# Attention probabilities of a hybrid encoder: one slot per head pair, turned as rounded words, values in one run

## The chip, the cores and the metric

The kernel runs on one core of a Trainium2 chip. The metric is the device time of one launch in microseconds (us); lower is better. TensorE (in profiles PE, its weight loads PEld) does the matmuls, VectorE is DVE, ScalarE is ACT, GpSimd is POOL, and SyncE (SP) issues the transfers. A float32 tile can also be declared as "rounded" words (F32R in the code, fp32r in a profile): the same four bytes, which TensorE takes in a cheaper kind of matmul. A plain float32 matmul of the program stands in the trace as two instructions, a rounded one and a transposition as one.

## The reference

One layer of an encoder is applied to two requests, 256 and 1024 rows of 2048 features. The input projection feeds three groups: a state-space scan (ssd), windowed attention, and attention to a memory of 256 rows per request. Their results are projected back and added to the input. The change touches the two attentions:

```python
# window attention: 8 heads of 64, 2 key-value heads, |t-s| <= 128, ALiBi, a sink logit per head
logits = where(valid, s - slopes * dist, -inf)
m = maximum(max(logits, axis=-1), sk)
pr = exp(logits - m)
probs = pr / (sum(pr, axis=-1) + exp(sk - m))
o = einsum('bngrqk,bnkgd->bnqgrd', probs, vw)
...
# memory attention: 4 heads of 128, 256 memory rows
pm = softmax(sm, axis=-1)
o_mem = einsum('bhtm,bmhd->bthd', pm, mv) * silu(z_mem)
```

## The kernel before

**Main work.** The projections are split-precision matmuls: each weight tile is split into a rounded part `wh` (ACT, L206) and the rest `wl` (DVE, L207), the inputs `xH` and `xL` likewise, and three rounded matmuls (L258 to L260, L293 to L295, L1268 to L1270) are summed into the PSUM tiles `acc`. Weights come by transfers into `wraw` tiles. Rows are worked in ten tiles of 128 (tiles 0 to 7 one request, 8 and 9 the other) in two groups of five.

**Work beside it.** Everything else is written as generators, put into two lanes (`queue`, L138). After each block step of a projection `pump` (L158) takes steps from the lanes, at rates by the name of the projection (RATES, L32). The attention tiles, key preparation and memory attention are in lane 0, the ssd work in lane 1. So the attention's matmuls come in short runs between the projection's matmuls, on the same TensorE queue, in about the order in which they are written; the weight splits have a higher priority. Three PSUM buffers (tag "mix", L74) serve all of the work beside the projections.

**Window attention, `attn(t)` (L620).** A tile of 128 query rows sees `na` blocks of 128 keys: two for tiles 0, 7, 8 and 9, three for the other six. For each of four head numbers `rr`, one head for each of two key-value heads `kv`:

- `scores(rr)` (L663): POOL copies the two sink logits into a column of the tile `lg` (L665). Two rounded matmuls per kv give the scores in PSUM (`psc`, L671 and L672), DVE adds the distances and takes the extreme value into `lg` (L673), ACT makes the exponentials with their sum (L677), DVE scales by half the reciprocal (L681).
- `turn_(rr)` (L685): for each kv, `na` transpositions of `lg` on TensorE, as plain float32 words against `ident`, into a PSUM tile `ppt` (L693); then ACT copies that to `pT` (L694), before the next kv's transpositions are written.
- `values(half)` (L698): for two `rr` together, plain float32 matmuls of `v_all` (64 columns, so the two kv fill the two halves of the PSUM partitions) with `pT`, 256 columns each (L703), then one DVE multiplication by the gate `z` (L706).

The order of steps is: scores 0, 1, turn 0, scores 2, turn 1, scores 3, values 0, turn 2, turn 3, values 1, with yields between. `lg` has two buffers that rotate, so scores 2 must wait until turn 0 has read its buffer; `pT` has one buffer for two `rr`.

**Memory attention, `mem_attn(t)` (L734),** is built alike with two head pairs `hp`: exponentials and scaling in `mpr` (L781, L786; the buffers of `lg`), four transpositions per `hp` (L794, plain words, PSUM tile `pmt`), an ACT copy to `mpT` (L798; the buffer of `pT`), and values for each `hp` (L809, 128 columns into all 128 partitions).

**Neighbours that the prediction uses.** The queries are turned as rounded words against `identr` (L653, PSUM tile `pq`, four to a run). The ssd work has plain matmuls of 128 columns into 64 partitions, the two halves of the partitions in turn, 32 instructions to a run (L970, PSUM tile `py`), and plain transpositions in fours (L1038, `pr`). `rsqrt` (L122) puts two small instructions on POOL. A table of row factors `rbc` for group 1 (L1463) also lives in a buffer of `lg`; it is last read at 603.7 us, ahead of the first transposition of `lg` at 637.5 us.

Of the kernel before, what the change touches and what calls it, by code (L numbers as in the profile page):

```python
# [10 lines left out]
F32 = mybir.dt.float32  # L11
F32R = mybir.dt.float32r
# [3 lines left out]
AF = mybir.ActivationFunctionType  # L16
ALU = mybir.AluOpType
AX = mybir.AxisListType

P = 128  # L20
# [24 lines left out]
def hymba_encoder_kernel(  # L45
# [37 lines left out]
    def psum(name):  # L83
        return mix.tile([P, 512], F32, tag="mix", name=name)
# [41 lines left out]
    def hv(ap, n=8):  # L126
        return ap.rearrange("p (h d) -> p h d", h=n)
# [48 lines left out]
    rbc = {}  # L176
# [440 lines left out]
        yield  # L617


    def attn(t):  # L620
        lo, hi = (0, NS) if t < NS else (NS, NT)
        k0, k1 = max(lo, t - 1), min(hi, t + 2)
        na = k1 - k0
        nk = na * P
        d0 = (k0 - (t - 1)) * P
        s0 = k0 if t < 4 else k0 - 3
        grp, ti = divmod(t, 5)
        tc_ = slice(ti * P, (ti + 1) * P)
        q = taken("attn", t)
        yield  # L630
        sq = w2("sq")
        A.activation(sq, q, AF.Square)
        ss = sm.tile([P, 8], F32, tag="s8", name="qss", bufs=4)
        V.reduce_sum(out=ss, in_=hv(sq), axis=AX.X)
        r = sm.tile([P, 8], F32, tag="s8", name="qr", bufs=4)
        rsqrt(r, ss, 1.0 / 64, 8)
        G.tensor_tensor(out=r, in0=r, in1=steep, op=ALU.mult)
        for _ in range(3):
            yield
        q3 = hv(q)  # L640
        V.tensor_mul(q3, q3, hb(r, 8, 64))
        yield
        qT = []
        for b in range(2):
            qh = mp.tile([P, 4, 2, 64], F32R, tag="wa", name="qh", bufs=WA)
            qb = q3[:, 4 * b:4 * b + 4, :]
            A.activation(qh[:, :, 0, :], qb, AF.Copy)
            V.tensor_sub(qh[:, :, 1, :], qb, qh[:, :, 0, :].bitcast(F32))
            yield
            ps = psum("pq")  # L650
            qf = qh.rearrange("p a b d -> p (a b d)")
            for a in range(4):
                T.transpose(ps[:, a * P:(a + 1) * P].bitcast(F32R), qf[:, a * P:(a + 1) * P], identr)  # L653
            o = mp.tile([P, 512], F32R, tag="qT", name="qT", bufs=2)
            A.activation(o, ps, AF.Copy)
            qT.append(o)
        z = w2("za")
        S.dma_start(hv(z, 4), zT_d[0][grp][:, :, tc_])
        yield
        ns8 = nsink.rearrange("p (v r) -> p r v", v=2)  # L660
        state_ = {}

        def scores(rr):  # L663
            lg = mp.tile([P, 2, 385], F32, tag="lg", name="lg", bufs=2)
            G.tensor_copy(lg[:, :, nk:nk + 1], ns8[:, rr, :].unsqueeze(2))  # L665
            nm = sm.tile([P, 2], F32, tag="m2", name="nm", bufs=10)
            for kv in range(2):
                h = 4 * kv + rr
                ps = psum("psc")
                st = qT[kv][:, rr * P:(rr + 1) * P]  # L670
                T.matmul(ps[:, :nk], st, kT[:, kv, s0 * P:s0 * P + nk], start=True, stop=False)  # L671
                T.matmul(ps[:, :nk], st, kL[:, kv, s0 * P:s0 * P + nk], start=False, stop=True)  # L672
                V.tensor_tensor_reduce(out=lg[:, kv, :nk], in0=pdist[:, d0:d0 + nk], in1=ps[:, :nk], scale=2.0 ** -(h + 1),  # L673
                                       scalar=nsink[:, h:h + 1], op0=ALU.add, op1=ALU.min, accum_out=nm[:, kv:kv + 1])
            den = sm.tile([P, 2], F32, tag="m2", name="den", bufs=10)
            for kv in range(2):
                A.activation(lg[:, kv, :nk + 1], lg[:, kv, :nk + 1], AF.Exp, scale=-1.0, bias=nm[:, kv:kv + 1],  # L677
                             accum_out=den[:, kv:kv + 1])
            V.reciprocal(out=den, in_=den)
            for kv in range(2):  # L680
                V.tensor_scalar(out=lg[:, kv, :nk], in0=lg[:, kv, :nk], scalar1=den[:, kv:kv + 1], scalar2=0.5,  # L681
                                op0=ALU.mult, op1=ALU.mult)
            state_[rr] = lg

        def turn_(rr):  # L685
            lg = state_.pop(rr)
            if rr % 2 == 0:
                state_["pT"] = mp.tile([P, 2, 2, 384], F32, tag="pT", name="pT", bufs=1)
            pT = state_["pT"]
            for kv in range(2):  # L690
                pt = psum("ppt")
                for a in range(na):
                    T.transpose(pt[:, a * P:(a + 1) * P], lg[:, kv, a * P:(a + 1) * P], ident)  # L693
                A.activation(pT[:, kv, rr % 2, :nk], pt[:, :nk], AF.Copy)  # L694

        oT = w2("oT")

        def values(half):  # L698
            pT = state_.pop("pT")
            po = psum("po")  # L700
            for a in range(na):
                for kv in range(2):
                    T.matmul(hv(po[kv * 64:kv * 64 + 64, :2 * P], 2), v_all[:, s0 + a, kv * 64:kv * 64 + 64],  # L703
                             pT[:, kv, :, a * P:(a + 1) * P], start=(a == 0), stop=(a == na - 1))
            c = slice(half * 2 * P, (half + 1) * 2 * P)
            V.tensor_mul(oT[:, c], po[:, :2 * P], z[:, c])  # L706

        scores(0)
        yield
        scores(1)  # L710
        yield
        yield
        turn_(0)
        yield
        scores(2)
        yield
        turn_(1)
        yield
        scores(3)
        yield  # L720
        values(0)
        yield
        turn_(2)
        yield
        turn_(3)
        yield
        fetch_next()
        yield
        values(1)
        yield  # L730
        S.dma_start(oT_d[0][grp][:, :, tc_], hv(oT, 4))


    def mem_attn(t):  # L734
# [31 lines left out]
        def scores(hp):  # L766
            ps = psum("pms")
            for j in range(2):
                h = 2 * hp + j
                c = slice(h * P, (h + 1) * P)  # L770
                o = ps[:, j * 256:(j + 1) * 256]
                T.matmul(o, qh[:, c], mkH[:, h, :], start=True, stop=False)
                T.matmul(o, qh[:, c], mkL[:, h, :], start=False, stop=False)
                T.matmul(o, ql[:, c], mkH[:, h, :], start=False, stop=True)
            m = sm.tile([P, 2], F32, tag="m2", name="mm", bufs=10)
            V.reduce_max(out=m, in_=hv(ps, 2), axis=AX.X)
            V.scalar_tensor_tensor(out=m, in0=m, scalar=-1.0, in1=r[:, 2 * hp:2 * hp + 2], op0=ALU.mult, op1=ALU.mult)
            pr = mp.tile([P, 512], F32, tag="lg", name="mpr", bufs=2)
            den = sm.tile([P, 2], F32, tag="m2", name="mden", bufs=10)
            for j in range(2):  # L780
                A.activation(pr[:, j * 256:(j + 1) * 256], ps[:, j * 256:(j + 1) * 256], AF.Exp,  # L781
                             scale=r[:, 2 * hp + j:2 * hp + j + 1], bias=m[:, j:j + 1], accum_out=den[:, j:j + 1])
            V.reciprocal(out=den, in_=den)
            for j in range(2):
                c = slice(j * 256, (j + 1) * 256)
                V.tensor_scalar(out=pr[:, c], in0=pr[:, c], scalar1=den[:, j:j + 1], scalar2=0.5,  # L786
                                op0=ALU.mult, op1=ALU.mult)
            st_[hp] = pr

        def turn_(hp):  # L790
            pr = st_[hp]
            pt = psum("pmt")
            for a in range(4):
                T.transpose(pt[:, a * P:(a + 1) * P], pr[:, a * P:(a + 1) * P], ident)  # L794
            if hp == 0:
                st_["pT"] = mp.tile([P, 2, 768], F32, tag="pT", name="mpT", bufs=1)
            pT = st_["pT"][:, hp, :512]
            A.activation(pT, pt, AF.Copy)  # L798
            st_[hp] = pT

# [658 lines left out]
    def x_rows(grp):  # L1459

        yield
        yield
        rbc[grp] = fin.tile([P, 640], F32, tag="rbc", name="rbc") if grp == 0 else \  # L1463
            mp.tile([P, 640], F32, tag="lg", name="rbc", bufs=2)
        for o, n in ((0, 4), (4, 1)):
            ps = psum("prx")
            for i in range(n):
                t = 5 * grp + o + i
                T.matmul(ps[:, i * P:(i + 1) * P], rx[:, t:t + 1].broadcast_to([P, P]), ident, start=True, stop=True)
            V.tensor_copy(rbc[grp][:, o * P:(o + n) * P], ps[:, :n * P])  # L1470
        yield
# [289 lines left out]
```

## Time and profile before

| | us |
|---|---|
| median of 3 runs | 1787.72 (1787.32 to 1790.27) |
| profiled execution, first to last instruction | 1784.2 |
| TensorE busy in it | 1774.6 |
| VectorE busy | 1245.8 |
| ScalarE busy | 921.5 |
| GpSimd busy | 547.3 |
| window attention's transpositions | 637.5 to 1303.8 |
| memory attention's transpositions | 828.6 to 1466.8 |

The profile describes one execution, whose own time isn't recorded beyond its span. In a timeline row the columns are: start in us from the span's start, duration in us, engine, line of the kernel, operation, the tile written and the tiles read, partitions and elements, and the count of merged instructions. Matmul durations overlap: the next one starts before the last one ends. In a row by groups, "busy, mean ns of one" stands behind the first bar, and behind the second the idle time of the engine just before these instructions with what ended it.

### The profile page before, as it was taken

What the parts mean: (1) busy time and instruction counts of PE and PEld (TensorE: products, weight loads), DVE (VectorE), ACT (ScalarE), POOL (GpSimd) and SP (SyncE); (2) the same over time, 40 slices, a digit from 0 to 9 for tenths busy, and PEclk for the clock granted to TensorE, in tenths of its full rate; (3) what the DMA queues carried; (4) which work ended last, traced back from release to release, by engine and by line L of the source; (5) the groups of instructions that cost most, each with busy time, mean ns of one, the idle gap of its engine ahead of it and who ended that gap; (6) DMA issues with size and microseconds to landing.
All of it is one profiled execution on the core that took longest, in us unless ns stands there. A gap on an engine that the chain in (4) does not pass through costs nothing.

```text
span 1784.2 us, 31407 instructions
## 1 busy us (share of the span) xinstructions
PE 1774.6 (99%) x10838; PEld 1606.3 (90%) x10838; DVE 1245.8 (70%) x2358; ACT 921.5 (52%) x2049; POOL 547.3 (31%) x900
## 2 busy tenths in 40 slices
PE   9999999999999999999999999999999999999999
PEld 7889999999998999999889977877988888899999
DVE  5596788888768887777665666557777644766665
ACT  5555455555434766756464565544447533533333
POOL 0105789999810100001001010000100000057775
PEclk9999999999999999999999999999999999999999
DMA  8654454445446644453635645557777764744442
GB/s 299 191 183 125 135 154 148 141 146 159 126 144 205 199 134 139 135 162 110 189 118 175 193 148 160 168 158 249 229 229 242 247 189 140 224 147 142 148 142 78
DMA packets 208207, 301.12 MB, mean 169 GB/s; under 512 B 19568, under 2 KB 86192, under 8 KB 208048
## 3 DMA queue, kind: packets, MB, share of 16 engines
q1 hardware_dynamic: 207904, 299.06, 54.5%
q8 instruction: 85, 1.39, 0.3%
q14 instruction: 74, 0.61, 0.1%
q10 hardware_dynamic: 144, 0.06, 0.0%
HBM read 236.36 MB, written 62.69 MB: 168 GB/s over the span
## 4 chain that ended last, share of the span: by engine, by line
PE 82%; issue 6%; DVE 4%; DMA 4%; POOL 2%; ACT 1%; SPq 0%; POOLq 0%; ACTq 0%; DVEq 0%
PE acc L258 9%; PE acc L260 8%; PE acc L259 8%; PE acc L1268 7%; PE acc L1270 7%; PE acc L1269 7%; PE acc L293 5%; PE acc L295 5%; PE acc L294 5%; PE accm L1268 3%; PE accm L1269 3%; PE accm L1270 3%; PE po L703 1%; PE ppt L693 1%; PE py L970 1%
## 5 line engine op out<-in xcount | busy, mean ns | idle before, releaser
L207 DVE TENSOR_TENSOR wl<-wraw,wh 128x512 fp32r<-128x512 f32 (+1 forms) x480 | 346.2, 723 | 244.0 <-ACT wh L206 238.5
L206 ACT ACTIVATE wh<-wraw 128x512 fp32r<-128x512 f32 (+1 forms) x480 | 292.2, 613 | 312.4 <-PE acc L260 147.8
L258 PE MATMUL acc<-wh,xH 128*128 128x512 f32 (+1 forms) x1088 | 418.9, 385 | 0.4 <-DVE v_all L337 0.4
L260 PE MATMUL acc<-wh,xL 128*128 128x512 f32 (+1 forms) x1088 | 410.1, 377 | 0.0
L259 PE MATMUL acc<-wl,xH 128*128 128x512 f32 (+1 forms) x1088 | 409.7, 377 | 0.0
L258 PEld LDWEIGHTS acc<-wh,xH 128*128 128x128 f32 x1088 | 204.5, 188 | 37.8 <-issue 3.4
L260 PEld LDWEIGHTS acc<-wh,xL 128*128 128x128 f32 x1088 | 204.4, 188 | 37.0 <-issue 0.2
L259 PEld LDWEIGHTS acc<-wl,xH 128*128 128x128 f32 x1088 | 204.7, 188 | 35.9 <-issue 1.6
L293 PE MATMUL acc<-xH,wh 128*128 128x320 f32 x640 | 202.8, 317 | 0.0
L294 PE MATMUL acc<-xL,wh 128*128 128x320 f32 x640 | 198.8, 311 | 0.0
L295 PE MATMUL acc<-xH,wl 128*128 128x320 f32 x640 | 198.0, 309 | 0.0
L206 ACT ACTIVATE sh<-ws 128x384 fp32r<-128x384 f32 x176 | 91.3, 523 | 204.8 <-POOL ws L1236 102.5
L207 DVE TENSOR_TENSOR sl<-ws,sh 128x384 fp32r<-128x384 f32 x176 | 123.8, 706 | 94.6 <-ACT sh L206 94.4
L1236 POOL TENSOR_TENSOR ws<-wraw 128x128 f32<-128x128 f32 x176 | 110.8, 630 | 205.8 <-DMA wraw<-in_w_in_pairs_dram 80.9
L665 POOL COPY lg<-nsink 128x2 f32<-128x2 f32 x40 | 13.6, 340 | 379.1 <-PE ppt L693 221.3
L1236 POOL TENSOR_TENSOR ws<-wraw,ws 128x128 f32<-128x128 f32 x176 | 118.7, 674 | 13.8
L293 PEld LDWEIGHTS acc<-xH,wh 128*128 128x128 f32 x640 | 120.2, 188 | 2.8 <-issue 2.2
L294 PEld LDWEIGHTS acc<-xL,wh 128*128 128x128 f32 x640 | 120.3, 188 | 1.7 <-issue 1.4
L295 PEld LDWEIGHTS acc<-xH,wl 128*128 128x128 f32 x640 | 120.2, 188 | 0.6 <-issue 0.5
L1236 POOL TENSOR_TENSOR wraw<-wraw 128x128 f32<-128x128 f32 x176 | 112.9, 642 | 13.7
L1236 POOL TENSOR_TENSOR ws<-ws,wraw 128x128 f32<-128x128 f32 x176 | 115.6, 657 | 0.0
L362 DVE SCALAR_TENSOR_TENSOR c<-u,vec,c 128x638 f32<-128x638 f32 (+1 forms) x96 | 90.0, 938 | 9.9 <-ACT c L357 9.5
(437 smaller groups left out, 3942.7 us busy)
## 6 DMA issues: line engine op xcount, KB each, us to landing
wraw<-in_w_in_laid_dram SPq DMA_DIRECT2D x176, 256.0 KB, 3.0
wraw<-in_w_in_pairs_dram SPq DMA_DIRECT2D x112, 256.0 KB, 2.7
wraw<-in_w_out_laid_dram SPq DMA_DIRECT2D x64, 256.0 KB, 3.5
wraw<-in_w_out_pairs_dram SPq DMA_DIRECT2D x64, 256.0 KB, 2.8
rf<-ac SPq DMA_DIRECT2D x40, 256.0 KB, 4.1
rb<-ac SPq DMA_DIRECT2D x40, 256.0 KB, 4.7
wraw<-in_w_mem_laid_dram SPq DMA_DIRECT2D x32, 256.0 KB, 4.4
xst<-in_x_sample_dram SPq DMA_DIRECT2D x20, 256.0 KB, 5.9
```

The lines of the kernel that those rows point to most:

```text
L206: a = A.activation(h, raw, AF.Copy)
L207: b = V.tensor_sub(l, raw, h.bitcast(F32))
L258: T.matmul(ps[t][:, :n], sh, h[:, :n], start=(k_ == 0), stop=False)
L259: T.matmul(ps[t][:, :n], sh, l[:, :n], start=False, stop=False)
L260: T.matmul(ps[t][:, :n], sl, h[:, :n], start=False, stop=(k_ == KT - 1))
L293: T.matmul(o, sh, cur["H", q][:, m, c], start=(k == 0), stop=False)
L294: T.matmul(o, sh, cur["L", q][:, m, c], start=False, stop=False)
L295: T.matmul(o, sl, cur["H", q][:, m, c], start=False, stop=(k == KT - 1))
L1236: G.tensor_tensor(out=o, in0=x, in1=y, op=op)
L1268: T.matmul(ps[p], h, xh, start=(k_ == 0), stop=False)
L1269: T.matmul(ps[p], h, xl, start=False, stop=False)
L1270: T.matmul(ps[p], l, xh, start=False, stop=(k_ == 7))
```

## The change

Scores, their rounded-kind words and their turned form share one slot of SBUF: there are four slots (tags lg0 to lg3) of one buffer each, one for each `rr` (two of them for the two `hp`), in place of two buffers of `lg` and one of `pT`. The scaled probabilities are transposed as F32R words against `identr`: a tile `lgw` of that type is taken in the same slot, POOL writes one word per partition of it (behind the columns that are transposed), and each transposition is made to wait for the DVE instruction that wrote the words. Both kv's transpositions are written first, then both ACT copies, into a tile `pT` in the same slot. The values of a window-attention tile are made in one run at its end, with 128 columns to a matmul, and multiplied by the gate in one DVE instruction; the step that held the first half is now an empty yield. Memory attention keeps its two values steps; its slots and transpositions change alike. The table `rbc` of group 1 takes slot 3.

```diff
+    def slot(i, name, shape, dtype=F32):
+        return mp.tile([P] + shape, dtype, tag=f"lg{i}", name=name, bufs=1)
+    WRITTEN = mybir.DependencyInfo(mybir.DependencyClass.Sync, mybir.DependencyReason.DATA)
+    def turn_words(out, words, wrote):
+        i = T.transpose(out.bitcast(F32R), words, identr)
+        for w in wrote:
+            tc.add_manual_dep(i.ins, w.ins.name, WRITTEN, reason="the words' writer")
+    def as_words(i, name, shape):
+        w = slot(i, name, shape, F32R)
+        G.memset(w.bitcast(F32)[(slice(None),) + tuple(slice(n - 1, n) for n in shape)], 0.0)
+        return w
...
         def scores(rr):
-            lg = mp.tile([P, 2, 385], F32, tag="lg", name="lg", bufs=2)
+            lg = slot(rr, "lg", [2, 385])
...
         def turn_(rr):
-            lg = state_.pop(rr)
-            if rr % 2 == 0:
-                state_["pT"] = mp.tile([P, 2, 2, 384], F32, tag="pT", name="pT", bufs=1)
-            pT = state_["pT"]
+            wrote = state_.pop(rr)
+            lg = as_words(rr, "lgw", [2, 385])
+            pts = []
             for kv in range(2):
                 pt = psum("ppt")
+                pts.append(pt)
                 for a in range(na):
-                    T.transpose(pt[:, a * P:(a + 1) * P], lg[:, kv, a * P:(a + 1) * P], ident)
-                A.activation(pT[:, kv, rr % 2, :nk], pt[:, :nk], AF.Copy)
+                    turn_words(pt[:, a * P:(a + 1) * P], lg[:, kv, a * P:(a + 1) * P], wrote[kv:kv + 1])
+            pT = state_["pT", rr] = slot(rr, "pT", [2, 385])
+            for kv in range(2):
+                A.activation(pT[:, kv, :nk], pts[kv][:, :nk], AF.Copy)
...
-        def values(half):
-            pT = state_.pop("pT")
+        def values():
             po = psum("po")
-            for a in range(na):
-                for kv in range(2):
-                    T.matmul(hv(po[kv * 64:kv * 64 + 64, :2 * P], 2), v_all[:, s0 + a, kv * 64:kv * 64 + 64],
-                             pT[:, kv, :, a * P:(a + 1) * P], start=(a == 0), stop=(a == na - 1))
-            c = slice(half * 2 * P, (half + 1) * 2 * P)
-            V.tensor_mul(oT[:, c], po[:, :2 * P], z[:, c])
+            for rr in range(4):
+                pT = state_.pop(("pT", rr))
+                for a in range(na):
+                    for kv in range(2):
+                        T.matmul(po[kv * 64:kv * 64 + 64, rr * P:(rr + 1) * P], v_all[:, s0 + a, kv * 64:kv * 64 + 64],
+                                 pT[:, kv, a * P:(a + 1) * P], start=(a == 0), stop=(a == na - 1))
+            V.tensor_mul(oT, po, z)
...
-            pr = mp.tile([P, 512], F32, tag="lg", name="mpr", bufs=2)
+            pr = slot(hp, "mpr", [512])
...
         def turn_(hp):
-            pr = st_[hp]
+            wrote = st_[hp]
+            pr = as_words(hp, "mprw", [513])
             pt = psum("pmt")
             for a in range(4):
-                T.transpose(pt[:, a * P:(a + 1) * P], pr[:, a * P:(a + 1) * P], ident)
-            if hp == 0:
-                st_["pT"] = mp.tile([P, 2, 768], F32, tag="pT", name="mpT", bufs=1)
-            pT = st_["pT"][:, hp, :512]
+                turn_words(pt[:, a * P:(a + 1) * P], pr[:, a * P:(a + 1) * P], wrote[a // 2:a // 2 + 1])
+            pT = slot(hp, "mpT", [512])
             A.activation(pT, pt, AF.Copy)
...
-            mp.tile([P, 640], F32, tag="lg", name="rbc", bufs=2)
+            slot(3, "rbc", [640])
```

More of the change, by code (lines that the diff above doesn't have):

```diff
@@ L679, in scores @@
             V.reciprocal(out=den, in_=den)
-            for kv in range(2):
-                V.tensor_scalar(out=lg[:, kv, :nk], in0=lg[:, kv, :nk], scalar1=den[:, kv:kv + 1], scalar2=0.5,
-                                op0=ALU.mult, op1=ALU.mult)
-            state_[rr] = lg
+            wrote = [V.tensor_scalar(out=lg[:, kv, :nk], in0=lg[:, kv, :nk], scalar1=den[:, kv:kv + 1], scalar2=0.5,
+                                     op0=ALU.mult, op1=ALU.mult) for kv in range(2)]
+            state_[rr] = wrote
         def turn_(rr):
-            lg = state_.pop(rr)
-            if rr % 2 == 0:
-                state_["pT"] = mp.tile([P, 2, 2, 384], F32, tag="pT", name="pT", bufs=1)
-            pT = state_["pT"]
+            wrote = state_.pop(rr)
+            lg = as_words(rr, "lgw", [2, 385])
+            pts = []
             for kv in range(2):
                 pt = psum("ppt")
+                pts.append(pt)
                 for a in range(na):
-                    T.transpose(pt[:, a * P:(a + 1) * P], lg[:, kv, a * P:(a + 1) * P], ident)
-                A.activation(pT[:, kv, rr % 2, :nk], pt[:, :nk], AF.Copy)
+                    turn_words(pt[:, a * P:(a + 1) * P], lg[:, kv, a * P:(a + 1) * P], wrote[kv:kv + 1])
+            pT = state_["pT", rr] = slot(rr, "pT", [2, 385])
+            for kv in range(2):
+                A.activation(pT[:, kv, :nk], pts[kv][:, :nk], AF.Copy)
         oT = w2("oT")
-        def values(half):
-            pT = state_.pop("pT")
+        def values():
             po = psum("po")
-            for a in range(na):
-                for kv in range(2):
-                    T.matmul(hv(po[kv * 64:kv * 64 + 64, :2 * P], 2), v_all[:, s0 + a, kv * 64:kv * 64 + 64],
-                             pT[:, kv, :, a * P:(a + 1) * P], start=(a == 0), stop=(a == na - 1))
-            c = slice(half * 2 * P, (half + 1) * 2 * P)
-            V.tensor_mul(oT[:, c], po[:, :2 * P], z[:, c])
+            for rr in range(4):
[5 more added lines that the diff above has]
+            V.tensor_mul(oT, po, z)
         scores(0)
@@ L720, in attn @@
         yield
-        values(0)
         yield
@@ L728, in attn @@
         yield
-        values(1)
+        values()
         yield
@@ L783, in scores @@
             V.reciprocal(out=den, in_=den)
+            wrote = []
             for j in range(2):
                 c = slice(j * 256, (j + 1) * 256)
-                V.tensor_scalar(out=pr[:, c], in0=pr[:, c], scalar1=den[:, j:j + 1], scalar2=0.5,
-                                op0=ALU.mult, op1=ALU.mult)
-            st_[hp] = pr
+                wrote.append(V.tensor_scalar(out=pr[:, c], in0=pr[:, c], scalar1=den[:, j:j + 1], scalar2=0.5,
+                                             op0=ALU.mult, op1=ALU.mult))
+            st_[hp] = wrote
         def turn_(hp):
-            pr = st_[hp]
+            wrote = st_[hp]
+            pr = as_words(hp, "mprw", [513])
             pt = psum("pmt")
             for a in range(4):
-                T.transpose(pt[:, a * P:(a + 1) * P], pr[:, a * P:(a + 1) * P], ident)
-            if hp == 0:
-                st_["pT"] = mp.tile([P, 2, 768], F32, tag="pT", name="mpT", bufs=1)
-            pT = st_["pT"][:, hp, :512]
+                turn_words(pt[:, a * P:(a + 1) * P], pr[:, a * P:(a + 1) * P], wrote[a // 2:a // 2 + 1])
+            pT = slot(hp, "mpT", [512])
             A.activation(pT, pt, AF.Copy)
```

## Prediction

> **What bounds the kernel now.** I read the page first: busy times, slices, chain.
>
> ```profile
> span 1784.2 us, 31407 instructions
> PE 1774.6 (99%) x10838; PEld 1606.3 (90%) x10838; DVE 1245.8 (70%) x2358; ACT 921.5 (52%) x2049; POOL 547.3 (31%) x900
> PEclk9999999999999999999999999999999999999999
> PE 82%; issue 6%; DVE 4%; DMA 4%; POOL 2%; ACT 1%; SPq 0%; POOLq 0%; ACTq 0%; DVEq 0%
> ```
>
> TensorE has work in 99% of the span, at an undiminished clock, and makes up 82% of the chain that ended last. The attention work that the change touches has no stage of its own: its matmuls are set between the projection matmuls (tile acc), on one in-order queue. So a nanosecond more or less of PE time between two projection matmuls is a nanosecond of the kernel, as long as no other engine comes late. A busy time won't do as a price, because the matmuls overlap: I took prices from the timeline of PE, from starts alone. A run of attention matmuls between two acc matmuls costs the time from its first start to the start of the second acc matmul behind it, less one ordinary step of the acc matmuls. (The second, because the first one behind a run takes a longer step.)
>
> **Transpositions: 288 change their kind.** Today the probabilities are turned as plain words (L693, L794). Two lone runs, of six and of four:
>
> ```profile
> 702.30 0.31 PE L293 MATMUL acc<-xH,wh 128*128 128x320 f32 x1
> ...
> 702.74 0.82 PE L693 MATMUL ppt<-identr,lg 128*128 128x128 f32 x6
> 703.32 0.39 PE L293 MATMUL acc<-xH,wh 128*128 128x320 f32 x1
> 703.55 0.31 PE L294 MATMUL acc<-xL,wh 128*128 128x320 f32 x1
> ...
> 1496.47 0.60 PE L1038 MATMUL pr<-identr,yd 128*128 128x128 f32 x4
> 1496.82 0.47 PE L258 MATMUL acc<-wh,xH 128*128 128x512 f32 x1
> 1497.14 0.39 PE L259 MATMUL acc<-wl,xH 128*128 128x512 f32 x1
> ```
>
> The kernel also has transpositions of rounded words against the same identity; runs of four and of eight stand alone:
>
> ```profile
> 673.47 0.46 PE L653 MATMUL pq<-identr,qh 128*128 128x128 f32 x4
> 673.76 0.38 PE L293 MATMUL acc<-xH,wh 128*128 128x320 f32 x1
> 673.99 0.30 PE L294 MATMUL acc<-xL,wh 128*128 128x320 f32 x1
> ...
> 1065.84 0.79 PE L653 MATMUL pq<-identr,qh 128*128 128x128 f32 x8
> 1066.46 0.46 PE L258 MATMUL acc<-wh,xH 128*128 128x512 f32 x1
> 1066.77 0.39 PE L259 MATMUL acc<-wl,xH 128*128 128x512 f32 x1
> 1066.99 0.40 PE L260 MATMUL acc<-wh,xL 128*128 128x512 f32 x1
> ```
>
> An acc step is 0.147 us with 320 columns (three from 702.30 to 702.74) and 0.22 with 512 (1066.77 to 1066.99). Plain words: six cost 0.81 - 0.147 = 0.663, four 0.67 - 0.22 = 0.45, so 0.11 each. Rounded words: four cost 0.52 - 0.147 = 0.373, eight 0.93 - 0.22 = 0.71, so 0.084 for each further one, and six would cost 0.373 + 2 x 0.084 = 0.541. A turn of six gains 0.122 us, a turn of four 0.077. By the loops of attn, tiles 1 to 6 see three key blocks and the other four tiles two: 6 x 4 = 24 turns of six and 4 x 4 = 16 turns of four; mem_attn has 10 x 2 = 20 turns of four. Gain: 24 x 0.122 + 36 x 0.077 = **5.7 us**. Bounds: nothing, if the new layout (the second key-value head's rows begin at word 385) loses the advantage; 288 x (0.11 - 0.084) = 7.5 us if no run pays a fixed part. I take 5.7, since pq is the same instruction with the same identity.
>
> **Values: two runs become one, and each matmul becomes two of half the width.** Lone runs of today's values, of twelve and of eight instructions (256 columns into 64 partitions), and of the one place that already has the new shape (128 columns into 64 partitions, the two halves of the partitions in turn), L970:
>
> ```profile
> 759.22 0.31 PE L295 MATMUL acc<-xH,wl 128*128 128x320 f32 x1
> 759.45 1.52 PE L703 MATMUL po<-pT,v_all 128*64 128x256 f32 x12
> 760.90 0.41 PE L293 MATMUL acc<-xH,wh 128*128 128x320 f32 x1
> 761.15 0.31 PE L294 MATMUL acc<-xL,wh 128*128 128x320 f32 x1
> ...
> 1189.33 0.39 PE L260 MATMUL acc<-wh,xL 128*128 128x512 f32 x1
> 1189.65 1.08 PE L703 MATMUL po<-pT,v_all 128*64 128x256 f32 x8
> 1190.67 0.50 PE L258 MATMUL acc<-wh,xH 128*128 128x512 f32 x1
> 1191.00 0.39 PE L259 MATMUL acc<-wl,xH 128*128 128x512 f32 x1
> ```
>
> ```profile
> 955.50 0.31 PE L295 MATMUL acc<-xH,wl 128*128 128x320 f32 x1
> 955.74 1.97 PE L970 MATMUL py<-rb,xs 128*64 128x128 f32 x32
> 957.64 0.41 PE L293 MATMUL acc<-xH,wh 128*128 128x320 f32 x1
> 957.89 0.31 PE L294 MATMUL acc<-xL,wh 128*128 128x320 f32 x1
> ```
>
> These runs start late too, so I count from one ordinary step after the acc matmul in front. Twelve: 761.15 - 759.22 - 2 x 0.147 = 1.636. Eight: 1191.00 - 1189.33 - 2 x 0.22 = 1.23. The difference gives 0.1015 per instruction and a fixed 0.42 per run, whatever its length. L970's run of 32: 957.89 - 955.50 - 0.294 = 2.096, so (2.096 - 0.42) / 32 = 0.052 per instruction: half the columns, half the price. A plain matmul leaves two instructions in the trace (12 for 3 blocks x 2 heads), so a tile's values become 48 or 32. Three blocks: 0.42 + 48 x 0.052 = 2.92 against 2 x 1.636 = 3.27, a gain of 0.35. Two blocks: L970's own 2.10 against 2 x 1.23 = 2.46, a gain of 0.36. Together 6 x 0.35 + 4 x 0.36 = **3.5 us**: just the ten fixed parts saved. [...]
>
> ```profile
> L809 PE MATMUL pmo<-mpT,mv 128*128 128x128 f32 x160 | 20.3, 276 | 0.1
> ```
>
> That is 20.3 / 160 = 0.127 each; at this price 416 instructions would cost 416 x (0.127 - 0.052) = 31 us more. I take L970's price, whose shape and alternation are those of the new loop.
>
> [...]
>
> **One slot for scores, words and turned words.** This adds waits and takes some away. (a) Turned words are written over the words, so ACT's first copy of a turn (L694), which today starts behind the first head's transpositions, must wait for both heads'. Behind it on ACT queue the splits of weights (L206), which run buffers ahead of PE: I cost that at nothing, with ACT busy 52% as cover, and up to 0.2 us a turn were it gone. But the copy also frees the PSUM buffer, one of three. Scores that come right behind a turn wait for that today already:
>
> ```profile
> 686.62 0.82 PE L693 MATMUL ppt<-identr,lg 128*128 128x128 f32 x6
> 687.19 0.42 PE L671 MATMUL psc<-kT,qT 128*128 128x384 f32 x1
> 687.45 0.34 PE L672 MATMUL psc<-kL,qT 128*128 128x384 f32 x1
> 687.78 0.44 PE L671 MATMUL psc<-kT,qT 128*128 128x384 f32 x1
> ...
> 791.73 0.82 PE L693 MATMUL ppt<-identr,lg 128*128 128x128 f32 x6
> ...
> 792.84 0.44 PE L671 MATMUL psc<-kT,qT 128*128 128x384 f32 x1
> ```
>
> Three places in the timeline of PE are so (these are the first and the last). There the second head's scores will start 6 x 0.084 - 3 x 0.11 = 0.17 us later, and the turn's gain of 0.122 vanishes into the same wait: 3 x 0.29 = **0.9 us** lost. Bounds: zero, if the new order parts them; 6.8 us (40 x 0.17) and all gain of attn's turns, if every turn got such a neighbour. (b) POOL gets 60 memsets of one word a partition, and the transpositions wait by hand for DVE's scaling (L681), as they do today. The nearest row for a memset is POOL's copy of two words, below. I cost them at nothing: no transposition reads that word, and POOL is busy 31%. (c) Scores 2 and 3 no longer wait for turns 0 and 1; POOL's copy waited there, nobody on PE's path. Scores 0 of the next tile wait for the values of this one, several steps earlier. (d) DVE multiplies once with 512 columns instead of twice with 256; no DMA is moved. Both are off the path, under DVE's 30% idle.
>
> **Sum.** -5.7 - 3.5 + 0.9 = -8.3 us. The profiled span of 1784.2 becomes 1775.9. The record has no separate time for the profiled execution; its span lies 3.5 below the median 1787.72, and I keep that distance: 1787.7 - 8.3 = **1779.4 us**.
>
> **The rivals.**
>
> *Halved matmuls are bound by their number, not their columns.* Then each keeps a part of today's 0.1015. At the whole of it the values cost 416 x (0.1015 - 0.052) = 20.6 us more: 1800.0; the kernel is slower from 0.052 + (8.3 + 3.6) / 416 = 0.081 each. L970's row speaks against it, 32 of the halved kind in a row at 0.052. Chance 0.03. [...]
>
> *The shared slot eats the gain.* If each of the 40 attention turns pinned a later PE matmul to the later copy, their gain (24 x 0.122 + 16 x 0.077 = 4.2) is lost and 40 x 0.17 = 6.8 comes on top: -5.7 - 3.5 + 4.2 + 6.8 = +1.8, about 1789.5. For it: the rows at 686.62 and 791.73. Against: the run at 702.74 has only acc matmuls behind it, which need no such buffer. Chance 0.10.
>
> *The turning doesn't get faster.* If words at odd offsets turn at 0.11 each, 3.5 us of the values remain, less up to 0.5 in waits: about 1784.7, no change. The plain runs at 702.74 start half their words there and show no penalty; no row tests it for rounded words. Chance 0.05.
>
> *POOL becomes the gate, and the kernel slower.* If each turn waits for its memset, and that stands in POOL's in-order queue, PE stalls with all projection matmuls behind it.
>
> ```profile
> L665 POOL COPY lg<-nsink 128x2 f32<-128x2 f32 x40 | 13.6, 340 | 379.1 <-PE ppt L693 221.3 <-ACT wh L206 108.3 <-DVE cbd L866 24.2
> ```
>
> And who waited for the writers of the tile lg:
>
> ```profile
> who waited for it (us, times):
> ...
>   PEld ppt L693: 0.7, 1
> ```
>
> Such a small instruction takes 0.34 us. Sixty stalls of that length are 20.4 us: 1799.8. It decides from (8.3 + 3.6) / 60 = 0.198 us a turn. For it: POOL's queue waits long before some instructions, 379.1 us before these copies alone. Against: the last row has TensorE's transpositions waiting once, 0.7 us; the words are ready well ahead, so a memset issued behind the same writer has that time, and the 221.3 us of waiting for turns disappear with the change. Chance 0.07.
>
> **How the numbers follow.** The forecast has 0.73. Its own range is 1777 to 1783: below by two of the three bounds (no fixed part in the turns, -1.8, and scores that don't wait, -0.9), above for places where a run that stands beside another today stands alone tomorrow, or where PE's order falls out worse. What a measurement of this kernel can tell from no change is 0.2%, 3.6 us. Faster: the forecast's 0.73. Same: 0.10 for the slot and 0.05 for the turning, 0.15. Slower: POOL's 0.07, 0.03 for the number of matmuls, and 0.02 for turns that pin more than I priced, 0.12. The range reaches from 1776.5 to 1790, to take in the two cases without a change; it leaves out the three slower cases and the tails, under 2 in 10.
>
> **What would show it.** In the changed profile: lone runs of ppt with six take about 0.46 us to the next acc start (now 0.58), pmt with eight about 0.63; one po run per tile with 48 or 32 instructions, 2.7 or 1.9 us to the next acc start; PE's busy time down by about 8 us and still 99%; scores behind a turn wait some 0.2 us longer for ACT's copy in a handful of places. Wrong: ppt idle until a POOL memset; po at 60 ns or more per instruction; psc waiting for L694's successor in dozens of places; or PE's runs as forecast but the span not, with new idle time before acc matmuls.

## The result, and the profile after

| | us |
|---|---|
| before, median of 6 runs | 1787.68 (1787.32 to 1790.27) |
| changed, median of 6 runs | 1781.88 (1779.80 to 1783.35) |
| ratio, with 95% interval | 0.9966 (0.9955 to 0.9976) |
| profiled execution of the changed kernel, first to last instruction | 1780.5 (its own time 1782.24) |

The kernel is 5.8 us faster, 0.34% by the ratio; 8.3 us were forecast. The changed kernel's runs spread over 3.6 us, and that turns out to matter. (Of the experiments below, one run of e7 took 3836.2 us and stands in no median.) The page of the changed kernel:

```profile
span 1780.5 us, 31950 instructions
PE 1766.1 (99%) x11046; PEld 1611.0 (90%) x11046; DVE 1245.5 (70%) x2348; ACT 918.6 (52%) x2049; POOL 550.2 (31%) x960
```

PE's busy time fell by 8.5 us (1774.6 to 1766.1), the span only by 3.7 (1784.2 to 1780.5). So PE was without work for 14.4 us of the span where it had been for 9.6: of the work saved, 4.8 us came back as waiting. These are single executions, and that of before was a short one, so the difference of spans is smaller than that of medians: by the medians 2.5 us of the forecast are missing.

The turns and the values cost what the rows of before said. Timeline of PE, changed kernel: a lone turn of six (L628 is now the line of every transposition of words), a lone pair of memory turns, a lone run of values with three key blocks and one with two:

```profile
702.30 0.65 PE L628 MATMUL ppt<-identr,lgw 128*128 128x128 f32 x6
702.79 0.38 PE L293 MATMUL acc<-xH,wh 128*128 128x320 f32 x1
703.00 0.31 PE L294 MATMUL acc<-xL,wh 128*128 128x320 f32 x1
...
757.88 0.31 PE L295 MATMUL acc<-xH,wl 128*128 128x320 f32 x1
758.12 2.85 PE L723 MATMUL po<-pT,v_all 128*64 128x128 f32 x48
760.91 0.42 PE L293 MATMUL acc<-xH,wh 128*128 128x320 f32 x1
761.16 0.31 PE L294 MATMUL acc<-xL,wh 128*128 128x320 f32 x1
...
1184.80 0.39 PE L260 MATMUL acc<-wh,xL 128*128 128x512 f32 x1
1185.11 1.98 PE L723 MATMUL po<-pT,v_all 128*64 128x128 f32 x32
1187.02 0.50 PE L258 MATMUL acc<-wh,xH 128*128 128x512 f32 x1
1187.36 0.40 PE L259 MATMUL acc<-wl,xH 128*128 128x512 f32 x1
...
1368.22 0.79 PE L628 MATMUL pmt<-identr,mprw 128*128 128x128 f32 x8
1368.85 0.46 PE L258 MATMUL acc<-wh,xH 128*128 128x512 f32 x1
1369.15 0.39 PE L259 MATMUL acc<-wl,xH 128*128 128x512 f32 x1
```

By the prediction's rule of counting: six 0.70 - 0.147 = 0.55 (forecast 0.54), eight 0.93 - 0.22 = 0.71 (as the queries' eight), values 3.28 - 0.294 = 2.99 and 2.56 - 0.44 = 2.12 (2.92 and 2.10).

What came back is in the waits of PE, longest first. Before, then changed (engine, line, waited for: us in total, times, longest):

```profile
PE pmt L794 <- DVE mpr L786: 1.4, 2, 1.3
...
PE psc L671 <- ACT qT L655: 0.2, 1, 0.2
```

```profile
PE psc L689 <- ACT qT L673: 2.4, 1, 2.4
PE pst L914 <- ACT fh L928: 1.8, 1, 1.8
PE warm L1562 <- DVE zero L1560: 1.3, 1, 1.3
PE pmt L628 <- DVE mpr L805: 1.3, 1, 1.3
PE acc L1286 <- ACT qs L326: 0.8, 1, 0.8
PE psc L689 <- DVE nm L691: 0.7, 1, 0.7
```

Two are new: 2.4 us at the first scores of tile 1, which wait for ACT's copy of the turned queries, and 1.8 us in the ssd work (L914), which waits for ACT too. The timeline around the first (PE and ACT, changed kernel):

```profile
677.07 0.41 PE L689 MATMUL psc<-kT,qT 128*128 128x384 f32 x1
...
677.89 0.63 ACT L977 ACTIVATE rb<-rb 128x512 f32<-128x512 f32 x1 [1.55 <-DVE rb L976]
...
678.72 0.72 ACT L365 ACTIVATE u<-c 128x646 f32<-128x646 f32 x1
679.35 0.61 ACT L206 ACTIVATE wh<-wraw 128x512 fp32r<-128x512 f32 x1
...
679.87 0.57 ACT L673 ACTIVATE qT<-pq 128x512 fp32r<-128x512 f32 x1
...
680.50 0.44 PE L689 MATMUL psc<-kT,qT 128*128 128x384 f32 x1 [2.41 <-ACT qT L673]
```

Read it from the end: PE's scores of the second head wait for the copy qT, the copy stands in ACT's queue behind four instructions, and the first of these (the ssd work's exponential, L977) has waited 1.55 us for VectorE. No instruction of the change is in these rows; further back, at 660 us, one is (see the step that failed, below).

### The profile page after: what moved, and what is told of

Its sections match the earlier page's. It is cut to its first block, busy times and chain, and to the rows that moved or that the text cites. A ratio compares the mean times of both kernels' runs of the same rounds, so it can differ in the third digit from the quotient of the medians.

```text
span 1780.5 us, 31950 instructions
## 1 busy us (share of the span) xinstructions
PE 1766.1 (99%) x11046; PEld 1611.0 (90%) x11046; DVE 1245.5 (70%) x2348; ACT 918.6 (52%) x2049; POOL 550.2 (31%) x960
## 4 chain that ended last, share of the span: by engine, by line
PE 88%; DVE 5%; issue 3%; DMA 2%; ACT 1%; POOL 1%; SPq 0%; POOLq 0%; DVEq 0%; ACTq 0%
PE acc L258 11%; PE acc L260 10%; PE acc L259 10%; PE acc L1288 7%; PE acc L1286 7%; PE acc L1287 7%; PE acc L293 5%; PE acc L295 5%; PE acc L294 5%; PE accm L1287 3%; PE accm L1286 3%; PE accm L1288 3%; PE po L723 1%; PE py L988 1%; DVE wl L207 1%
## 5 line engine op out<-in xcount | busy, mean ns | idle before, releaser
L206 ACT ACTIVATE wh<-wraw 128x512 fp32r<-128x512 f32 (+1 forms) x480 | 292.1, 613 | 297.1 <-PE acc L260 150.5
L206 ACT ACTIVATE sh<-ws 128x384 fp32r<-128x384 f32 x176 | 91.2, 523 | 207.1 <-POOL ws L1254 103.4
L635 POOL MEMSET lgw<- 128x1 f32 x40 | 3.9, 98 | 315.9 <-DVE lg L698 227.0
```

The source lines that it names most:

```text
L206: a = A.activation(h, raw, AF.Copy)
```

## The experiments

The experiments ran in three groups (e1, e2, e3, e5; e6 to e9; e10 to e13), each beside its own runs of the kernel before, with medians of 1787.27, 1787.40 and 1786.84. Theory A: the PE work saved is as forecast, and a part comes back in waits of PE for ACT and VectorE, above all at 678 us. Rivals: the shared slot makes the waits, GpSimd does, or the merging of values is worth nothing.

| kernel | median us | ratio to before (95%) | wait of scores for qT, us |
|---|---|---|---|
| changed, first measurement | 1781.88 | 0.9966 (0.9955 to 0.9976) | 2.4 |
| e13 changed, again | 1782.46 | 0.9972 (0.9963 to 0.9981) | 2.7 |
| e1 plain words | 1788.55 | 1.0011 (1.0002 to 1.0019) | 3.0 |
| e2 two runs of values | 1782.01 | 0.9973 (0.9962 to 0.9985) | 0.7 |
| e3 three runs | 1783.25 | 0.9979 (0.9971 to 0.9988) | 0.6 |
| e5 slot per head, table overwritten | 1784.79 | 0.9993 (0.9984 to 1.0001) | 2.2 |
| e10 slot per head, table in the slots | 1781.96 | 0.9973 (0.9963 to 0.9982) | 2.1 |
| e6 wait for the memset | 1781.49 | 0.9964 (0.9952 to 0.9977) | 2.1 |
| e7 heads not in turn | 1784.29 | 0.9981 (0.9972 to 0.9991) | 2.1 |
| e9 copy of queries first | 1782.58 | 0.9975 (0.9966 to 0.9984) | 2.2 |
| e8 one more empty step | 1779.88 | 0.9955 (0.9943 to 0.9968) | 0.4 |
| e12 two runs, one more step | 1782.39 | 0.9970 (0.9961 to 0.9980) | none listed |
| e11 before, one more step | 1786.25 | 0.9994 (0.9985 to 1.0003) | 0.2 |

The last column is the longest such wait in the profiled execution. It sorts the kernels: with the values in one run at the tile's end and no added step it is 2.1 to 3.0 us, whatever else is changed; otherwise it is 0.7 or less.

**e1, plain words in the new slots.** The turning alone undone.

```diff
-            wrote = state_.pop(rr)
-            lg = as_words(rr, "lgw", [2, 385])
+            lg = state_.pop(rr)
...
-                    turn_words(pt[:, a * P:(a + 1) * P], lg[:, kv, a * P:(a + 1) * P], wrote[kv:kv + 1])
+                    T.transpose(pt[:, a * P:(a + 1) * P], lg[:, kv, a * P:(a + 1) * P], ident)
... (memory attention alike)
```

> The changed kernel (1781.9) with the turning alone undone: plain words against the plain identity, no memset, no wait by hand; slots and the single run of values stay. Theory A (PE work is the time; the turning is worth 5.7 us of it): PE busy 5 to 6 us more than in the changed kernel, runs of six back at 0.57 us to the next acc start, time about 1786 to 1787.6. Theory B (what the turning saves is lost in waits anyway): the same time as the changed kernel, within 2 us.

Measured 1788.55, which is 6.7 us above the changed kernel: the turning is worth its whole price, and theory B is out. PE is busy 1775.1 us, 9.0 more than in the changed kernel; this profile has two stretches of half clock of 3.4 us each, and without the 1.7 us that I estimate for each, 5.6 remain, the forecast 5.7. It also says something that I had not expected: slots and merged values alone, without the faster turning, are a little slower than before (by 1.3 us, in part by the clock: all of e1's 11 runs had less than the full clock, and 1 of 29 of the kernel before).

**e2 and e3, two and three runs of values.**

```diff
-        def values():
+        def values(half):
...
-            for rr in range(4):
+            for rr in (2 * half, 2 * half + 1):
...
         scores(3)
         yield
+        values(0)
         yield
...
-        values()
+        values(1)
```

> The changed kernel with its values in two runs at the places of before, matmuls still of 128 columns. Theory A (a run of values has a fixed cost of 0.42 us): ten runs more, 10 x 0.42 = 4.2 us, about 1786.1. Theory B (the gain of the values lies in the halved matmuls or in the waits around the run, not in the count of runs): the time of the changed kernel, about 1782.

> As the kernel with two runs, but three runs a tile (head number 0, 1, then 2 and 3). Theory A: twenty runs more than the changed kernel, 20 x 0.42 = 8.4 us, about 1790.3, slower than before. Theory B: about 1782.

By the time, theory A missed: 1782.01 and 1783.25. PE's work did rise:

```profile
PE 1768.8 (99%) x11046; PEld 1610.3 (90%) x11046; DVE 1246.0 (70%) x2358; ACT 920.0 (52%) x2049; POOL 554.4 (31%) x960
```

```profile
PE 1770.5 (99%) x11046; PEld 1610.8 (90%) x11046; DVE 1246.7 (70%) x2368; ACT 920.6 (52%) x2049; POOL 551.6 (31%) x960
```

That is 2.7 and 4.4 us over the changed kernel. But the wait at the first scores of tile 1 shrinks with it, to 0.7 and 0.6 us (the wait at L914 keeps 1.1 and 0.6). By the prediction's counting a lone run of 24 costs 759.51 - 757.55 - 0.294 = 1.67 us in e2, so two cost 3.33 and the merged run 2.99: 0.35 saved, as forecast. The reading to be tested by e12: merging saves PE work and opens that wait, and the two cancel.

**e5 and e10, a slot for each head,** so that ACT's first copy waits for its own head alone.

```diff
-            lg = slot(rr, "lg", [2, 385])
+            lg = [slot(f"{rr}{kv}", "lg", [385]) for kv in range(2)]
...
+                pT.append(slot(f"{rr}{kv}", "pT", [385]))
+                A.activation(pT[kv][:, :nk], pt[:, :nk], AF.Copy)
```

> The changed kernel with a slot for each head, so that ACT's first copy of a turn waits for its own head's transpositions only (memory attention gets two copies of 256 columns a turn in place of one of 512; the table of row factors moves out of the slots). Theory A (the shared slot costs a handful of 0.3 us waits): 1781 to 1782. Theory B (the shared slot is what eats some 2.5 us of the forecast): about 1779.

> A slot for each head again, with the table of row factors in two pieces in two of the slots (two VectorE instructions in place of one where it is read, before any score). Theory A (the wait at 678 us is for ACT's copy of the queries, not for the slots): that wait stays at some 2 us, time 1781 to 1783. Theory B (the shared slot eats the missing gain): the wait is gone, about 1779.

In e5 the table of row factors lay in the tile of the ssd state, which is written before the table's last use: group 1 is normalised with other numbers there, and its time carries the waits of that order. e10, with the table in two of the slots, computes all; it takes 1781.96, and the wait for qT stays at 2.1 us. So waiting for the other head's transpositions is not what eats the gain. The slots themselves are not cleared by this: in e10, too, only the single run of values frees them, and GpSimd's copies into those of the next tile wait 10.56 us for it (at 659.0 us).

**e6, transpositions also wait for GpSimd's memset.**

```diff
-                    turn_words(pt[:, a * P:(a + 1) * P], lg[:, kv, a * P:(a + 1) * P], wrote[kv:kv + 1])
+                    turn_words(pt[:, a * P:(a + 1) * P], lg[:, kv, a * P:(a + 1) * P], wrote[kv:kv + 1] + gate)
... (gate is the memset; memory attention alike)
```

> The changed kernel with each transposition of words also made to wait for its memset on GpSimd. Theory A (the memset takes 0.098 us right behind the words' writer and is long done): the same, within 1 us of 1781.9. The prediction's slower rival (GpSimd as the gate): from 12 us more, if each of 60 turns loses 0.2 us.

1781.49, the same: the memsets are no gate. In the changed kernel's profile the memset takes 0.098 us:

```profile
L635 POOL MEMSET lgw<- x40: 98/98/100, 634.7 to 1291.8; 128x1 f32 x40
```

**e7, the heads of the values not in turn** (the loops over `a` and `kv` exchanged).

> The changed kernel with the values of one key-value head after the other within a head number, so that the two halves of the partitions no longer alternate from matmul to matmul. Theory A (0.052 us per instruction comes from two halves that overlap): where two neighbours use the same half, each pays nearly twice, up to 0.11 per instruction, 416 x 0.055 = 23 us more at most, about 1795 to 1805. Theory B (0.052 is the price of 128 columns, overlap or not): the same time as the changed kernel.

1784.29, only 2.4 us over the changed kernel, with PE busy 2.7 us more (1768.8). Both theories of that expectation are too simple: a run of 48 takes longer, but by a tenth, not by a factor of two. Its group of instructions in the timeline of PE, beside the x48 row of the changed kernel above (2.85):

```profile
760.02 3.12 PE L723 MATMUL po<-pT,v_all 128*64 128x128 f32 x48
```

**e8, one more empty step ahead of the first scores,** and **e9, the copies of the queries at the priority of the weight splits.**

```diff
+        yield
         scores(0)
```

```diff
-            A.activation(o, ps, AF.Copy)
+            with tc.high_priority(offset=HP[2]):
+                A.activation(o, ps, AF.Copy)
```

> The changed kernel (1781.9) with one more empty step between the turned queries and the first scores of each window-attention tile, so that ACT's copies of the queries have a block step's time before TensorE needs them. Theory A (part of the forecast gain is given back in one wait of 2.4 us, where the scores of tile 1 wait for ACT's copy qT, with a dip of the clock behind it in some executions): the wait is gone, about 1779. Theory B (waits just move to the next place where another engine is late): the same as the changed kernel, 1781 to 1783.

> The changed kernel with ACT's copies of the turned queries at the priority of the weight splits, with no step added. Theory A: ACT no longer runs a wait for VectorE ahead of the copy at 678 us, about 1779. Theory B: ACT then waits for TensorE's transpositions in front of other work, and the time stays or rises, 1781 to 1784.

e8 takes 1779.88, 0.5 from the forecast of 1779.4. In the stretch from 676 to 690 us PE is busy all of the time. Rows of three kernels for that stretch (us, then busy time of PE, weight loads, DVE, ACT, POOL with counts, granted clock, DMA share, GB/s): the changed kernel, the changed kernel again (e13), and e8.

```profile
676.00:690.00 14.00, 11.54 (x80) 11.01 (x78) 11.50 (x31) 8.51 (x22) 0.20 (x2) 1.00 0.44 145
```

```profile
676.00:690.00 14.00, 11.33 (x58) 11.07 (x58) 8.92 (x25) 6.52 (x16) 0.10 (x1) 0.76 0.37 122
```

```profile
676.00:690.00 14.00, 14.00 (x96) 14.00 (x95) 10.69 (x29) 9.77 (x23) 0.20 (x2) 1.00 0.55 156
```

e9 moved nothing: in its timeline ACT still runs L978 (waiting 1.55 us for VectorE's L977), L972, L365 and L206 ahead of the copy, the order of the changed kernel, and the wait is 2.2 us. The edit didn't bring about what it was to test, so e9 says nothing on theory A.

**e11, before with the step; e12, two runs with the step; e13, the changed kernel again.**

> The kernel before, with the empty step ahead of the first scores and nothing else. Theory A (the step removes a wait that only the change had made long, 0.19 us before and 2.4 after): no change, within 1.5 us of before (1787.4). Theory B (the step itself paces the lanes better): about 1785, as much gained as in the changed kernel.

> The changed kernel with the empty step and with its values in two runs. Theory A (a run has a fixed cost of 0.33 to 0.42 us, which the wait hid in the kernel with two runs): 10 runs more than with the step alone (1779.9), about 1783.2 to 1784. Theory B (merging the runs gains nothing): about 1780.

> The changed kernel itself again, on the same chip as the three beside it: 1781 to 1783, with the wait of some 2 us at 678 us.

e11 is no faster than before within its interval: the step isn't a gain in itself. e12 lies between its two theories. It is 2.5 us slower than e8 (1782.39 against 1779.88), but not all of that is the merging: e12's profile has a wait of its own elsewhere,

```profile
PE pd L1095 <- ACT xH L197: 2.7, 1, 2.7
```

with a stretch of half clock of 3.4 us from 1281.9, and 5 of its 8 runs had less than the full clock. At full clock alone the medians are 1780.8 (3 runs) against e8's 1779.3 (4 runs). So with the wait for qT out of the way the kernel with the merged run is 1.5 to 2.5 us ahead (about 3 if each is set against before in its own group). How much of that is the merging isn't shown, as e12's own wait is of the same size. e13 repeats the changed kernel and shows something more beside its wait, in the middle row above: a granted clock of 0.76 in that stretch. The clock stands at half for 6.8 us there, from 678.8 on, the last 0.9 us of the wait included. e1 has 3.4 us of half clock from 685.1, 1.5 us behind its wait (3.0 us), and another at 152.7, behind two waits of 0.8 us each. Half clock for 3.4 us is 1.7 us of matmuls lost, by my estimate. At the mean clock of a whole run it shows in the third digit: of the changed kernel's 6 + 10 runs, 6 had 1.000 (medians 1781.2 and 1780.5 in the two measurements) and 10 less (1783.2 and 1782.7). e8 had 1.000 in 4 of 5, the kernel before in 18 of 21 and 26 of 31 in the last two groups.

## Why the prediction was right, and where its size was off

- **Turning: right.** Forecast 5.7 us; undone it costs 6.7 in time and, with the estimated loss by the clock taken off, 5.6 in PE work (e1). The lone turns cost what the queries' rows gave.
- **Values: the price right, the gain not kept in the kernel.** 2.99 and 2.12 us a run against 2.92 and 2.10. Where the scores don't wait, the kernels with and without merging lie 1.5 to 3 us apart (e8 and e12), with merging's share not shown; the changed kernel and e2 are level, because with merging PE comes to the queries' scores ahead of ACT. (The prediction calls its 3.5 "just the ten fixed parts saved"; ten of its 0.42 would be 4.2. The sum goes by 3.5.)
- **The step that failed** is the sum's premise, "as long as no other engine comes late", with two lines that put other engines at nothing: (d), ACT and VectorE "off the path, under DVE's 30% idle", and (c), where POOL's copies wait with "nobody on PE's path" and the next tile's scores wait for the values of this one "several steps earlier". The 30% is a mean over the span. The stretch from 662 to 676 us, before and changed (columns as for e8 above; VectorE is the one behind the weight loads, 13.42 and 11.57 of 14 us):

```profile
662.00:676.00 14.00, 14.00 (x96) 13.82 (x95) 13.42 (x24) 10.41 (x27) 0.00 (x0) 1.00 0.66 195
```

```profile
662.00:676.00 14.00, 14.00 (x97) 13.86 (x96) 11.57 (x23) 9.63 (x25) 2.76 (x5) 1.00 0.55 172
```

What VectorE lacks there is in the timelines: ACT squares tile 1's queries (sq), GpSimd makes the queries' factors from them (qr), and VectorE multiplies the queries by these. Before, then changed:

```profile
653.46 0.62 ACT L632 ACTIVATE sq<-q 128x512 f32<-128x512 f32 x1
...
654.97 0.57 POOL L123 TENSOR_SCALAR qr<-qss 128x8 f32<-128x8 f32 x1 [3.22 <-DVE qss L634]
...
660.09 0.68 DVE L641 TENSOR_TENSOR q<-q,qr 128x512 f32<-128x512 f32 x1
```

```profile
659.88 0.62 POOL L683 COPY lg<-nsink 128x2 f32<-128x2 f32 x2 [10.58 <-PE po L723]
...
662.27 0.63 ACT L650 ACTIVATE sq<-q 128x512 f32<-128x512 f32 x1
...
664.47 0.77 POOL L123 TENSOR_SCALAR qr<-qss 128x8 f32<-128x8 f32 x1 [2.32 <-DVE qss L652]
...
667.28 0.69 DVE L659 TENSOR_TENSOR q<-q,qr 128x512 f32<-128x512 f32 x1 [2.10 <-POOL qr L655]
```

In the changed kernel all four copies of sink logits into tile 1's slots stand ahead of the queries' factors on GpSimd, and they wait 10.58 us for the single run of values, which alone frees the slots. The factors begin 9.5 us later than before, and VectorE waits 2.10 us for them. From there to 677 us it waits at most 0.34 us more, so it is still behind when ACT waits for it at L977, ahead of qT. The kernels sort by this too: over the whole execution VectorE waits for these factors 15.4 to 19.3 us in every kernel with the values in one run, and 3.1 to 5.6 us in the others, where the factors begin ahead of the last of the copies. In e8 this waiting stays (18.9 us); its empty step gives ACT more time before the scores. The copies are not the whole cause: behind them GpSimd waits another 2.32 us for the squares, which ACT makes 8.8 us later than before, and why they stand so late in ACT's order no run shows.

The prediction named this way to be wrong last ("PE's runs as forecast but the span not") and gave it no price. It measured: 4.8 us more of PE without work in the profiled execution, 2.2 of them at one place, and a dip of the clock in many executions.
- **(a) The later first copy: not seen.** Forecast 0.9 us lost in three places. The changed profile's list of waits, which goes down to 0.2 us, has no scores behind a turn that wait for ACT's copy of it; where they follow a turn, as at 688 us, acc matmuls now stand between the two heads. e10 shows nothing to be had there.
- **(b) GpSimd: right** for the memsets, by e6; its copies of the sink logits are the ones that came late. **The number of matmuls: right**, 2.79 us to the next acc start for 48 is 0.058 each with all overheads.
- **The range** (1776.5 to 1790) and the direction held. That the time came as near as 2.5 us is in part luck: the 0.9 us taken off for (a) were not lost there, and stand in the sum in place of a part of the waits that it had at nothing. The wait of 1.8 us at L914 was not tested by itself (it is absent from e8's list).

## What to carry to other kernels

Price an instruction on the bound engine from start to start in a lone run, with the fixed cost of the run apart from the cost of one: these prices held to within 3%. Then go along the queue and ask at each meeting with another engine whether that engine is early enough to be met sooner; take its busy share from that stretch, not from the span. Where a buffer comes free later than it did, look at what stands in the queue behind the instruction that waits for it. One empty step at the right place gave back what the meeting cost: the version with it (e8) is the fastest here, 1779.88 us, 0.45% under before.

## What the hardware showed that was not expected

- Beside some waits of PE the clock stands at half. In the profiled executions half clock for 3.4 or 6.8 us came in or behind waits of 2.7 us (e13, e12), 3.0 and two of 0.8 (e1) and 1.5 (e5, at 853.7 us); waits of 2.1 to 2.4 us in the changed kernel, e6, e7, e9 and e10 left the clock full. So the length of the wait alone doesn't say whether the clock is halved, and what does isn't shown here. Between runs of the changed kernel with and without the full clock lie 2.0 and 2.2 us.
- Two halves of the partitions need not alternate from one matmul to the next: three of one half, then three of the other cost 0.27 us more per run of 48 (3.12 against 2.85).
